# The value projections of the last four mLSTM heads as seven products of 2x2 blocks in seven PSUM banks

## The chip, the cores and the metric

One core of one Trainium2 chip runs the whole kernel. The metric is the device time of one execution in microseconds. Times of single instructions come from one profiled execution. PE is TensorE, DVE is VectorE, ACT is ScalarE; PSUM, the memory that TensorE writes, has eight banks of 128 x 512 float32.

## The reference, cut to what matters

The model is a two-layer trunk over 512 tokens of width 2048: an mLSTM layer, then a layer of band attention. The change lies in the mLSTM layer, whose input projection feeds eight heads.

```python
h = modulate(rmsnorm(x, g_pre[l]), shift, scale)          # (512, 2048)
proj = h @ w_in                                            # all columns of the layer
qk = silu(causal_conv(proj[..., :A_V0], conv_w, conv_b))   # queries and keys, 256 columns a head each
v = proj[..., A_V0:A_O0]                                   # values, 512 columns a head
o = proj[..., A_O0:A_Z0]
z = proj[..., A_Z0:A_G0]
ht = mlstm_chunkwise(heads(q), heads(k), heads(v), li, lf)  # scores, weights, weights @ values, per head
y = sigmoid(o) * rmsnorm(ht, g_head) * silu(z)
return y @ w_out
```

For one head the values are `h` (512 x 2048) times 512 columns of `w_in`. That product is what the change computes in another way.

## The kernel before, in words

**Numbers.** Everything is float32. A matmul operand is split into a high part (a cast to the rounded matmul type, made by ACT) and a low part (the rest, one subtraction on DVE); `split`, line 203, makes both. `mm3` makes one product of three matmuls: high x high, high x low, low x high. All matmuls are issued at line 272.

**Weights.** They lie in DRAM in the order in which the kernel uses them, which `stream()` writes out: a list of pieces of up to 128 x 1024. `raw_load` brings a piece into one of three raw buffers (`wr`, 512 KB, on the SP queue). `wpiece` (line 232 on) takes the next piece and makes `wh` and `wl` from it, three buffers each. If it is asked for sums, it first makes sums and differences of the piece's 2x2 blocks (`ws`, lines 242 to 244: one subtraction of 512, an addition and a subtraction of 256 columns in a piece of two pairs) and splits these too (`wsh`, `wsl`, 768 columns, two buffers each).

**Seven products.** The tiles of `proj_s` (a head's two query tiles, its two key tiles, each gate tile of o with that of z, keys of the attention layer) treat two k-tiles, two column tiles and two token halves as 2x2 blocks and form their product with seven block products in place of eight. Four banks D, C, A, B gather them. The block sums of the input `h1` (`h1s`, made by `three_sums`) exist from head 3 on; the sum for the first of a pair's tiles overwrites the second half of `h1` itself. At the end, lines 366 to 375 empty the banks: one copy on ACT from D, then four additions of 256 and one of 512 and one of 256 columns on DVE.

**A head from the fifth on (h > HALF, heads 4 to 7).** In this order on TensorE: a tile pair of queries (`ps_dzq`, `ps_czq`, `ps_azq`, `ps_bzq`), a pair of keys, the values, four tile pairs of the gates (`zo`), the normaliser (`ps_d`) and the weighted values (`ps_n`), whose matmuls mix with those of the next head. Queries and keys go through the convolution (`cv`, three DVE steps each, lines 656 to 661) and are split (`qk`).

**The values.** `proj_b` makes four banks of 128 tokens x 512 columns (`ps_v`): the token tile is stationary, 512 weight columns move. There are eight weight pieces, each of two k-tiles. Since `h1` holds a sum in its second token half, `wpiece` makes one difference of the two k-tiles' weights (`diff`, line 249, 512 columns) for these heads, and the second k-tile's products for the token blocks 2 and 3 use it. While the values run, four scores (`scores`, `ps_s`) are computed at given places (`at`), each in one bank of the second pool; DVE empties each at line 738 or 743. The values' banks are then split into `v` 0 to 2 (high by ACT, low by DVE, straight from PSUM) and copied to `v` 3.

**Banks.** Two pools share the eight banks: `newp` has five (psP), `newa` three (psA). A tile's name does not bind it to a bank; the recording layer gives it a bank that is free in its pool. `other` in `proj_s` says whether C, A and B come from `newa`.

**Order.** A scheduler puts the instructions of each engine in an order when the program is built; each engine then works through its own queue in that order and waits on semaphores. `tc.high_priority(AHEAD)` draws instructions forward: weight pieces and the emptying of banks have it, the convolutions of heads 4 to 7 have not.

Of the kernel before, what the change touches and what calls it, by code (L numbers as in the profile page):

```python
# [15 lines left out]
P = 128  # L16
D = 2048
# [27 lines left out]
RAMP = [4, 5, 6, 7]  # L45
HALF = 3
ATT_PAIRS = 8


def pair_pieces(f, merged=False):  # L50
# [22 lines left out]
def stream():  # L73

    out = []

    def add(mat, kts, cs):
        out.append((mat, [(k, c, n) for k in kts for c, n in cs]))

    def tile_a(mat, col, kts=KT):  # L80
        for k in range(0, kts, 8):
            add(mat, range(k, k + 8), [(col, P)])

    def tile_b(mat, col, kts=KT):
        for k in range(0, kts, 2):
            add(mat, [k, k + 1], [(col, 512)])

    def tile_s(mat, c1, c2, f, merged=False):
        for sk, nk in pair_pieces(f, merged):
            blocks = [(2 * k + i, c, P) for ks in sk for i, c in ((0, c1), (0, c2), (1, c2), (1, c1)) for k in ks]  # L90
            out.append((mat, blocks + [(2 * k + i, c, P) for k in nk for i in range(2) for c in (c1, c2)]))

    for step in first_steps():
        if len(step) == 1:
            add("a_w_in", step, [(c, P) for c in LEAD])
        else:
            k0, k1, i, g = step
            add("a_w_in", range(k0, k1), [(c, P) for c in LATER[i : i + g]])
    for h in range(NH):
        for c in (h * DK, V0 // 2 + h * DK):  # L100
            if 1 < h <= HALF:
                tile_a("a_w_in", c)
                tile_a("a_w_in", c + P)
            elif h > HALF:
                tile_s("a_w_in", c, c + P, HEAD_PAIRS, True)
        tile_b("a_w_in", V0 + h * DV)
        if h >= HALF:
            for i in range(4):
                tile_s("a_w_in", O0 + h * DV + i * P, Z0 + h * DV + i * P, HEAD_PAIRS if h > HALF else RAMP[i], True)
        elif h:  # L110
            for c0 in (O0, Z0):
                for i in range(4):
                    tile_a("a_w_in", c0 + h * DV + i * P)
    tile_b("a_w_out", 0, 32)
    for _ in PAIRS:
        for g in range(1, 4):
            tile_b("a_w_out", g * 512, 32)
    for _ in PAIRS:
        for g in range(2):
            tile_b("kv_w", D + g * 512)  # L120
    for i in range(KT // 2):
        tile_s("kv_w", 2 * i * P, (2 * i + 1) * P, KEY_PAIRS[i], True)
    for g in range(2, 4):
        tile_b("kv_w", D + g * 512)
    for h in range(BH):
        tile_s("b_w_in", h * P, D + h * P, ATT_PAIRS, True)
    for g in range(3):
        tile_b("b_w_out", g * 512)
    for _ in PAIRS:
        tile_b("b_w_out", 3 * 512)  # L130
    return out
# [15 lines left out]
def hybrid_trunk(ctx, tc, xT, xN, c, adaT, cols, wst, wg, ext, kc, out):  # L147
# [71 lines left out]
        keep(nc.sync.dma_start(raw, wst[at : at + P * n].rearrange("(p n) -> p n", p=P)))  # L219
        loads.append(raw)  # L220

    def wpiece(mat, groups=(), pl=None, bufs=(2, 2), diff=False, early=False):

        if stock and not early:
            return stock.pop(0)()
        i = wpos[0] - len(loads)
        m, blocks = order[i]
        assert m == mat  # L230
        n = sum(w for _, _, w in blocks)
        with tc.high_priority(ahead[0]):
            if not loads:
                raw_load()
            raw = loads.pop(0)
            ts = []
            c0 = 0
            for j, ns in enumerate(groups):
                w = ns * P
                r = raw[:, c0 : c0 + 4 * w]  # L240
                t = pl.tile([P, 3 * w], F32, tag="ws", name=f"ws{i}_{j}", bufs=bufs[0])
                nc.vector.tensor_tensor(t[:, : 2 * w], r[:, w : 3 * w], r[:, : 2 * w], op=ALU.subtract)  # L242
                nc.vector.tensor_tensor(r[:, w : 2 * w], t[:, w : 2 * w], r[:, :w], op=ALU.add)  # L243
                nc.vector.tensor_tensor(t[:, 2 * w :], r[:, 3 * w :], r[:, w : 2 * w], op=ALU.subtract)  # L244
                ts.append(t)
                c0 += 4 * w
            if diff:
                t = pl.tile([P, n // 2], F32, tag="ws", name=f"ws{i}", bufs=2)
                nc.vector.tensor_tensor(t, raw[:, n // 2 :], raw[:, : n // 2], op=ALU.subtract)
                ts.append(t)  # L250
            hi = wp.tile([P, 1024], F32R, tag="hi", name=f"wh{i}")[:, :n]
            lo = wp.tile([P, 1024], F32R, tag="lo", name=f"wl{i}")[:, :n]
            if i == 0:
                pin(nc.scalar.copy(hi, raw))

                def rest():
                    parted[0] = nc.vector.tensor_tensor(lo, raw, hi.bitcast(F32), op=ALU.subtract)
                    behind(parted[0], first[0])
                    return [(hi, lo)]

                return rest
            parted[:] = split(hi, lo, raw, *first[1:] if i < 3 else ())
            out = [(hi, lo)]
            for j, t in enumerate(ts):
                sh = pl.tile(list(t.shape), F32R, tag="wsh", name=f"wsh{i}_{j}", bufs=bufs[1])
                sl = pl.tile(list(t.shape), F32R, tag="wsl", name=f"wsl{i}_{j}", bufs=bufs[1])
                split(sh, sl, t)
                out.append((sh, sl))
        return out
# [20 lines left out]
    def proj_a(mat, xs, ps, t0=0, t1=S):  # L290
        proj(mat, xs, [ps], 8, 0, len(xs), len(xs) - 1, t0, t1)

    def proj_b(mat, xs, pss, ms=range(4), kts=KT, at={}, late=0, summed=0, pl=None):

# [1 line left out]
        for k0 in range(0, kts, 2):  # L298
            if k0 in at:
                at[k0]()  # L300
            held.append((k0, wpiece(mat, pl=pl, diff=k0 < 2 * summed)))
            if k0 >= kts - 2 * late and k0 < kts - 2:
                continue
            for group in [[pm] for pm in zip(pss, ms)] if k0 in (0, kts - 2) else [list(zip(pss, ms))]:
                for ka, parts in held:
                    for j in range(2):
                        k = ka + j
                        x = xs(k) if callable(xs) else xs[k]
                        for ps, m in group:
                            t = slice(m * P, (m + 1) * P)  # L310
                            other = j == 1 and m > 1 and len(parts) > 1
                            w = slice(0, 512) if other else slice(j * 512, (j + 1) * 512)
                            hi, lo = parts[other]
                            mm3(ps, x[:, 0, t], x[:, 1, t], hi[:, w], lo[:, w], k == 0, k == kts - 1)
            held.clear()

    def proj_s(mat, xs, ss, f, z1, z2, name, pl, bufs, at={}, merged=False, other=False):

        D, C, A, B = [(newa if other and n != "d" else newp)(f"ps_{n}{name}") for n in "dcab"]
        pieces = pair_pieces(f, merged)
        begun = set()
        h0, h1_ = slice(0, 256), slice(256, 512)
# [40 lines left out]
        with tc.high_priority(AHEAD):  # L365
# [7 lines left out]
                nc.vector.tensor_tensor(z2, z2, B.rearrange("p (a t) -> p a t", a=2), op=ALU.add)  # L373
            else:
                nc.vector.tensor_tensor(z2[:, 0, :], z2[:, 0, :], B[:, h0], op=ALU.add)

    def half_sums(raw, pl, tag, name, bufs, keep=lambda ins: ins):

# [334 lines left out]
            raw.append(r)  # L713
        h1s.append(three_sums(raw, hq, f"h1s{k}", HEAD_PAIRS, h1[2 * k][:, :, 256:]))

    def pair(c, name, other, f=HEAD_PAIRS, at={}):
        z1, z2 = (acp.tile([P, 2, 256], F32, tag="so", name=f"{name}_{i}", bufs=6) for i in range(2))
        proj_s("a_w_in", h1, h1s, f, z1, z2, name, hq, (2, 2), at, True, other)
        return [z.rearrange("p a t -> p (a t)") for z in (z1, z2)]

    def scores(h, j, qk, pr, nm, nmd, tot):
# [30 lines left out]
    for h in range(NH):  # L752
# [4 lines left out]
        for i in range(4):  # L757
            if h > HALF:
                if i % 2 == 0:
                    zs = pair((i // 2) * (V0 // 2) + h * DK, f"zq{h}_{i}", i > 0)  # L760
                ps = zs[i % 2]
            elif h < 2:
                ps = (lead, qk1)[h][i]
# [28 lines left out]
            add_at(at, {k: lambda: background(2) for k in ((4, 10) if h == 0 else (2, 6, 12))})  # L792
        if h == HALF:
            add_at(at, {k: head_sums for k in (2, 6, 10, 14)})
        pv = [newp(f"ps_v{h}_{m}") for m in range(4)]
        proj_b("a_w_in", h1, pv, at=at, summed=HEAD_PAIRS if h > HALF else 0, pl=hq if h > HALF else None)
        for i in (2 * h, 2 * h + 1):
            pin(nc.sync.dma_start(bsc[i], ext[i].partition_broadcast(P)))
        if h == 0:
# [4 lines left out]
        for m in range(4):  # L804
            with tc.high_priority(AHEAD):
                if m < 3:
                    t = hp.tile([P, 2, S], F32R, tag="qk", name=f"v{h}_{m}", bufs=4)
                    split(t[:, 0, :], t[:, 1, :], pv[m])
                else:
                    t = hp.tile([P, S], F32, tag="nm", name=f"v{h}_{m}")  # L810
                    nc.scalar.copy(t, pv[m])
# [5 lines left out]
        for i in range(4):  # L817
            if h >= HALF:
                f = HEAD_PAIRS if h > HALF else RAMP[i]
                o, sz = pair(O0 + h * DV + i * P, f"zo{h}_{i}", i % 2 == 0, f, {1: head_sums} if len(h1s) == f < HEAD_PAIRS else {})  # L820
                nc.scalar.activation(o, o, AF.Sigmoid)
                nc.scalar.activation(sz, sz, AF.Silu)
                nc.vector.tensor_tensor(o, o, sz, op=ALU.mult)
# [273 lines left out]
    for i in range(KT // 2):  # L1097
# [1 line left out]
        ready = len(hs)  # L1099
        at = {2: input_sums} if ready < KT // 2 else {}  # L1100
        assert ready == KEY_PAIRS[i]
        proj_s("kv_w", hkv, hs, ready, z[:, 0:2, :], z[:, 2:4, :], f"k{i}", zx, (2, 2), at, True, i % 2 == 1)
        nc.sync.dma_start(ksc[i].rearrange("p a t -> p (a t)"), z.rearrange("p a t -> p (a t)"))
    zxst.close()
    kst.close()
# [281 lines left out]
```

## Time and profile before

| | |
|---|---|
| median of 3 runs | 2770.73 us (2770.47 to 2773.43) |
| the profiled execution | 2771.84 us, of which the span of the trace is 2770.1 us |
| granted TensorE clock | 0.999 |
| one head's period, from the values of head 5 to those of head 6 | 1003.2 to 1180.0 us of the span, 176.8 us |
| matmuls in the span | 16402, with as many weight loads |

A row of the timeline begins with its start and its length in us, then engine, line, operation, output<-inputs, shapes; a bracket tells how long the engine had been idle before it and who ended that. A row of a chain has start, length, and the number of instructions that it stands for. A matmul's listed length is longer than the distance to the next one, since matmuls are pipelined; the spacing of starts tells what a product occupies.

### The profile page before, as it was taken

The numbers are of one execution on the slowest core, as the hardware profiler recorded it, in microseconds if no ns is written. First come the engines' busy times: TensorE is split into PE (matmuls) and PEld (weight loads), VectorE is DVE, ScalarE is ACT, GpSimd is POOL, SyncE is SP. The second block draws the span as 40 slices with busy tenths as digits, with TensorE's granted clock in tenths as the row PEclk, the third lists the DMA queues.
The fourth block names the chain that finished last, engine by engine and source line by source line (L and its number), as shares of the span: only waits on it lengthen the run. The fifth ranks groups of instructions, "written<-read, shape, count | busy, mean of one in ns | idle before, by whom it ended". The sixth has DMA issues, their size and how long they took to land.

```text
span 2770.1 us, 42407 instructions
## 1 busy us (share of the span) xinstructions
PE 2749.6 (99%) x16402; PEld 2451.6 (89%) x16402; DVE 2199.7 (79%) x3438; ACT 1399.4 (51%) x2000; POOL 0.2 (0%) x4
## 2 busy tenths in 40 slices
PE   8999999999999999999999999999999999999998
PEld 6887888888998999989999888887998899999877
DVE  8975978769997888978887677467976788899666
ACT  4243624234555555556555334468534466666523
POOL 0000000000000000000000000000000000000000
PEclk9999999999999999999999999999999999999999
DMA  9754687855233333333326699788535544444687
GB/s 368 292 204 131 249 301 259 312 202 204 101 114 107 99 124 100 115 103 105 124 94 221 223 297 310 237 273 279 176 129 189 169 129 129 126 123 126 211 311 243
DMA packets 167876, 527.08 MB, mean 190 GB/s; under 512 B 17989, under 2 KB 33893, under 8 KB 155001
## 3 DMA queue, kind: packets, MB, share of 16 engines
q1 hardware_dynamic: 167674, 524.38, 56.1%
q8 instruction: 128, 2.10, 0.3%
q14 instruction: 74, 0.61, 0.1%
HBM read 490.69 MB, written 38.85 MB: 191 GB/s over the span
## 4 chain that ended last, share of the span: by engine, by line
PE 93%; DVE 3%; DMA 2%; issue 1%; ACT 1%; SPq 0%; DVEq 0%; ACTq 0%
PE ps_y L272 18%; PE ps_v L272 12%; PE ps_kv L272 4%; PE ps_azo L272 4%; PE ps_o L272 4%; PE ps_czo L272 4%; PE ps_dzo L272 4%; PE ps_az L272 3%; PE ps_cz L272 3%; PE ps_dz L272 3%; PE ps_qk L272 3%; PE ps_z L272 3%; PE ps_l L272 3%; PE ps_bzo L272 2%; PE ps_s L272 2%; PE ps_n L272 2%
## 5 line engine op out<-in xcount | busy, mean ns | idle before, releaser
L203 DVE TENSOR_TENSOR wl<-wr,wh 128x1024 fp32r<-128x1024 f32 (+1 forms) x560 | 673.8, 1206 | 290.6 <-ACT wh L203 288.8
L203 ACT CAST wh<-wr 128x1024 fp32r<-128x1024 f32 (+1 forms) x560 | 579.8, 1037 | 625.5 <-PE ps_y L272 233.1
L272 PE MATMUL ps_y<-wh,y 128*128 128x512 f32 x1536 | 476.3, 390 | 0.0
L203 ACT CAST wsh<-ws 128x768 fp32r<-128x768 f32 (+2 forms) x240 | 189.1, 788 | 394.6 <-issue 170.3
L272 PEld LDWEIGHTS ps_y<-wh,y 128*128 128x128 f32 x1536 | 288.1, 188 | 59.3
L272 PE MATMUL ps_y<-wl,y 128*128 128x512 f32 x768 | 299.0, 389 | 0.0
L203 DVE TENSOR_TENSOR wsl<-ws,wsh 128x768 fp32r<-128x768 f32 (+2 forms) x240 | 215.3, 897 | 104.5 <-ACT wsh L203 102.5
L272 PE MATMUL ps_v<-wh,h 128*128 128x512 f32 x896 | 285.4, 390 | 0.0
L443 DVE CUSTOM_DVE_ANT_0 ada<-ada,scB,cl 128x2048 f32<-128x2048 f32 (+1 forms) x96 | 222.5, 2324 | 13.6 <-DMA ada<-in_adaT 13.6
L272 PEld LDWEIGHTS ps_v<-wh,h 128*128 128x128 f32 x896 | 168.2, 188 | 34.4
L272 PE MATMUL ps_v<-wl,h 128*128 128x512 f32 x448 | 174.7, 390 | 0.0
L272 PEld LDWEIGHTS ps_y<-wl,y 128*128 128x128 f32 x768 | 144.2, 188 | 29.8
L272 PE MATMUL ps_kv<-wh,hkv 128*128 128x512 f32 x512 | 159.4, 390 | 0.0
L242 DVE TENSOR_TENSOR ws<-wr 128x512 f32<-128x512 f32 (+1 forms) x208 | 138.9, 668 | 4.1 <-DMA wr<-in_wst 3.9
L272 PEld LDWEIGHTS ps_kv<-wh,hkv 128*128 128x128 f32 x512 | 96.1, 188 | 19.7
L272 PE MATMUL ps_kv<-wl,hkv 128*128 128x512 f32 x256 | 100.0, 390 | 1.4 <-DVE wl L203 1.4
L272 PEld LDWEIGHTS ps_v<-wl,h 128*128 128x128 f32 x448 | 84.2, 188 | 17.4 <-issue 0.9
L272 PE MATMUL ps_l<-h,wh 128*128 128x512 f32 x320 | 98.4, 390 | 0.0
L244 DVE TENSOR_TENSOR ws<-wr 128x256 f32<-128x256 f32 (+1 forms) x208 | 85.8, 413 | 3.4
L243 DVE TENSOR_TENSOR wr<-ws,wr 128x256 f32<-128x256 f32 (+1 forms) x208 | 85.4, 411 | 2.6
L272 PE MATMUL ps_qk<-h,wh 128*128 128x512 f32 x256 | 79.3, 390 | 0.0
L272 PE MATMUL ps_o<-h,wh 128*128 128x512 f32 x256 | 79.2, 389 | 0.0
(405 smaller groups left out, 6411.7 us busy)
## 6 DMA issues: line engine op xcount, KB each, us to landing
wr<-in_wst SPq DMA_DIRECT2D x530, 512.0 KB, 3.7
ada<-in_adaT SPq DMA_DIRECT2D x94, 1024.0 KB, 6.1
ada<-in_adaT SPq DMA_DIRECT2D x36, 512.0 KB, 6.3
adq<-in_adaT SPq DMA_DIRECT2D x64, 256.0 KB, 5.0
xt<-nsc SPq DMA_DIRECT2D x48, 256.0 KB, 4.3
wr<-in_wst SPq DMA_DIRECT2D x26, 384.0 KB, 3.3
yr<-ysc SPq DMA_DIRECT2D x28, 256.0 KB, 5.3
bsc<-in_ext SPq DMA_DIRECT2D x16, 320.0 KB, 6.1
```

The source lines that it names most:

```text
L203: ins = nc.scalar.copy(hi, src), nc.vector.tensor_tensor(lo, src, hi.bitcast(F32), op=ALU.subtract)
L242: nc.vector.tensor_tensor(t[:, : 2 * w], r[:, w : 3 * w], r[:, : 2 * w], op=ALU.subtract)
L243: nc.vector.tensor_tensor(r[:, w : 2 * w], t[:, w : 2 * w], r[:, :w], op=ALU.add)
L244: nc.vector.tensor_tensor(t[:, 2 * w :], r[:, 3 * w :], r[:, w : 2 * w], op=ALU.subtract)
L272: return nc.tensor.matmul(ps, a, b, start=start, stop=stop)
L443: pin(nc.vector.tensor_tensor_reduce(c, c, (sc or scB)[:, j * w : (j + 1) * w], 1.0, mod[:, i : i + 1] if j else col(CB + i), ALU.mult, AL ...
```

## The change: what it does

In heads 4 to 7 the values go through a new function, `proj_v`, in place of `proj_b`:

- the two k-tiles of a piece, the two halves of the 512 value columns and the two halves of the tokens are the 2x2 blocks; each block product is 128 tokens (stationary) by 256 columns (moving), with seven products in place of eight;
- 128 tokens of each half make one sub-block b; its banks are D, C, A, and both sub-blocks share a bank E, one half each: seven banks. Those of sub-block 0 and E come from `newp`, and so does C of sub-block 1; D and A of sub-block 1 come from `newa`, so that one bank is left for the four scores;
- the first two pieces and the last two are held: sub-block 0 takes both, then sub-block 1;
- `wpiece` makes the three block sums of a tile pair for each piece, and the difference of line 249 goes;
- the banks are emptied by additions into SBUF tiles, and `split` then reads these; `v` 3 is written directly;
- the score places move from k-tile 8, 10, 12, 14 to piece 4, 5, 6, 7, which is the same place in the stream;
- the four banks of a gate pair in these heads come from the pools as `OZ_BANKS` says.

```diff
+BANKS = ("pppp", "paaa")
+OZ_BANKS = ("pppa", "aapp", "paaa", "pppp")
...
+    def tile_v(mat, col):
+        for k in range(0, KT, 2):
+            c1, c2 = col, col + 256
+            out.append((mat, [(k + i, c, 256) for i, c in ((0, c1), (0, c2), (1, c2), (1, c1))]))
...
-        tile_b("a_w_in", V0 + h * DV)
+        if h > HALF:
+            tile_v("a_w_in", V0 + h * DV)
+        else:
+            tile_b("a_w_in", V0 + h * DV)
...
-            if diff:
-                t = pl.tile([P, n // 2], F32, tag="ws", name=f"ws{i}", bufs=2)
-                nc.vector.tensor_tensor(t, raw[:, n // 2 :], raw[:, : n // 2], op=ALU.subtract)
-                ts.append(t)
...
+    def proj_v(mat, xs, ss, zs, name, pl, bufs, at={}):
+        h0, h1_ = slice(0, 256), slice(256, 512)
+        E = newp(f"ps_e{name}")
+        banks = [[new(f"ps_{n}{name}_{b}") for n, new in zip("dca", news)] for b, news in enumerate(([newp] * 3, [newa, newp, newa]))]
+        begun = set()
+        n = KT // 2
+        held = []
+        def products(b, k, main, extra):
+            D, C, A = banks[b]
+            tok = slice(b * P, (b + 1) * P)
+            for ps, half, parts, blk, x in (
+                (D, 1, main, 1, ss[k][1]),
+                (D, 0, main, 0, xs[2 * k][:, :, h0]),
+                (C, 0, extra, 1, ss[k][2]),
+                (C, 1, extra, 0, ss[k][0]),
+                (A, 0, main, 3, xs[2 * k + 1][:, :, h0]),
+                (A, 1, main, 2, ss[k][3]),
+                (E, b, extra, 2, xs[2 * k + 1][:, :, h1_]),
+            ):
...
+                mm3(ps[:, h1_ if half else h0], x[:, 0, tok], x[:, 1, tok], parts[0][:, w], parts[1][:, w], start, bool(last))
+        def empty(b):
+            D, C, A = banks[b]
+            z0, z1 = zs(b)
+            f0, f1 = h0, h1_
+            with tc.high_priority(AHEAD):
+                nc.scalar.copy(z0[:, f0], D[:, h0])
+                nc.vector.tensor_tensor(z1[:, f1], z0[:, f0], D[:, h1_], op=ALU.add)
+                nc.vector.tensor_tensor(z1[:, f0], z1[:, f1], C[:, h0], op=ALU.add)
+                nc.vector.tensor_tensor(z0[:, f1], z1[:, f1], C[:, h1_], op=ALU.add)
+                nc.vector.tensor_tensor(z1[:, f1], z1[:, f0], C[:, h1_], op=ALU.add)
+                nc.vector.tensor_tensor(z0, z0, A, op=ALU.add)
+            return z0, z1
+        out = []
+        for k in range(n):
+            if k in at:
+                at[k]()
+            held.append((k, *wpiece(mat, [2], pl, bufs)))
+            if k in (0, n - 2):
+                continue
+            for b in range(2):
+                for piece in held:
+                    products(b, *piece)
+                if k == n - 1:
+                    out.append(empty(b))
+            held.clear()
+        for z, e in zip(out, (h0, h1_)):
+            with tc.high_priority(AHEAD):
+                nc.vector.tensor_tensor(z[1][:, h0], z[1][:, h0], E[:, e], op=ALU.add)
+        return [z[a] for a in range(2) for z in out]
...
+        if h > HALF:
+            def rows_of(b):
+                t = [acp.tile([P, S], F32, tag="so", name=f"zv{h}_{b}_{a}", bufs=6) for a in range(2 - b)]
+                return t + [hp.tile([P, S], F32, tag="nm", name=f"v{h}_3")] if b else t
+            pv = proj_v("a_w_in", h1, h1s, rows_of, f"v{h}", hq, (2, 2), {k // 2: f for k, f in at.items()})
+        else:
+            pv = [newp(f"ps_v{h}_{m}") for m in range(4)]
+            proj_b("a_w_in", h1, pv, at=at)
...
+                elif h > HALF:
+                    t = pv[m]
...
-                o, sz = pair(O0 + h * DV + i * P, f"zo{h}_{i}", i % 2 == 0, f, ...)
+                o, sz = pair(O0 + h * DV + i * P, f"zo{h}_{i}", OZ_BANKS[i] if h > HALF else BANKS[1 - i % 2], f, ...)
```

In the built program TensorE has 576 matmuls more (336 for 192 in each of four heads), DVE 112 instructions more (28 a head), and the order on every engine is the same as before outside the stretch from the values of head 4 to the first gate pairs of head 7. The tiles of the value stage are called `ps_dv`, `ps_cv`, `ps_av`, `ps_ev` and `zv`.

More of the change, by code (lines that the diff above doesn't have):

```diff
@@ L220, in raw_load, with wpiece @@
         loads.append(raw)
-    def wpiece(mat, groups=(), pl=None, bufs=(2, 2), diff=False, early=False):
+    def wpiece(mat, groups=(), pl=None, bufs=(2, 2), early=False):
         if stock and not early:
@@ L291, in proj_a, with proj_b @@
         proj(mat, xs, [ps], 8, 0, len(xs), len(xs) - 1, t0, t1)
-    def proj_b(mat, xs, pss, ms=range(4), kts=KT, at={}, late=0, summed=0, pl=None):
+    def proj_b(mat, xs, pss, ms=range(4), kts=KT, at={}, late=0):
         held = []
@@ L300, in proj_b @@
                 at[k0]()
-            held.append((k0, wpiece(mat, pl=pl, diff=k0 < 2 * summed)))
+            held.append((k0, wpiece(mat)))
             if k0 >= kts - 2 * late and k0 < kts - 2:
@@ L304, in proj_b @@
             for group in [[pm] for pm in zip(pss, ms)] if k0 in (0, kts - 2) else [list(zip(pss, ms))]:
-                for ka, parts in held:
+                for ka, [(hi, lo)] in held:
                     for j in range(2):
@@ L310, in proj_b, with proj_s @@
                             t = slice(m * P, (m + 1) * P)
-                            other = j == 1 and m > 1 and len(parts) > 1
-                            w = slice(0, 512) if other else slice(j * 512, (j + 1) * 512)
-                            hi, lo = parts[other]
+                            w = slice(j * 512, (j + 1) * 512)
                             mm3(ps, x[:, 0, t], x[:, 1, t], hi[:, w], lo[:, w], k == 0, k == kts - 1)
             held.clear()
-    def proj_s(mat, xs, ss, f, z1, z2, name, pl, bufs, at={}, merged=False, other=False):
-        D, C, A, B = [(newa if other and n != "d" else newp)(f"ps_{n}{name}") for n in "dcab"]
+    def proj_s(mat, xs, ss, f, z1, z2, name, pl, bufs, at={}, merged=False, banks="pppp"):
+        D, C, A, B = [(newa if b == "a" else newp)(f"ps_{n}{name}") for n, b in zip("dcab", banks)]
         pieces = pair_pieces(f, merged)
@@ L375, in proj_s @@
                 nc.vector.tensor_tensor(z2[:, 0, :], z2[:, 0, :], B[:, h0], op=ALU.add)
+    def proj_v(mat, xs, ss, zs, name, pl, bufs, at={}):
[17 more added lines that the diff above has]
+            ):
+                start = id(ps) not in begun
+                begun.add(id(ps))
+                w = slice(blk * 256, (blk + 1) * 256)
+                last = k == n - 1 and (b if ps is E else ps is not D and half or ps is D and not half)
+                mm3(ps[:, h1_ if half else h0], x[:, 0, tok], x[:, 1, tok], parts[0][:, w], parts[1][:, w], start, bool(last))
[28 more added lines that the diff above has]
+        return [z[a] for a in range(2) for z in out]
@@ L714, in head_sums, with pair @@
         h1s.append(three_sums(raw, hq, f"h1s{k}", HEAD_PAIRS, h1[2 * k][:, :, 256:]))
-    def pair(c, name, other, f=HEAD_PAIRS, at={}):
+    def pair(c, name, banks, f=HEAD_PAIRS, at={}):
         z1, z2 = (acp.tile([P, 2, 256], F32, tag="so", name=f"{name}_{i}", bufs=6) for i in range(2))
-        proj_s("a_w_in", h1, h1s, f, z1, z2, name, hq, (2, 2), at, True, other)
+        proj_s("a_w_in", h1, h1s, f, z1, z2, name, hq, (2, 2), at, True, banks)
         return [z.rearrange("p a t -> p (a t)") for z in (z1, z2)]
@@ L759, in hybrid_trunk @@
                 if i % 2 == 0:
-                    zs = pair((i // 2) * (V0 // 2) + h * DK, f"zq{h}_{i}", i > 0)
+                    zs = pair((i // 2) * (V0 // 2) + h * DK, f"zq{h}_{i}", BANKS[i // 2])
                 ps = zs[i % 2]
@@ L794, in hybrid_trunk @@
             add_at(at, {k: head_sums for k in (2, 6, 10, 14)})
-        pv = [newp(f"ps_v{h}_{m}") for m in range(4)]
-        proj_b("a_w_in", h1, pv, at=at, summed=HEAD_PAIRS if h > HALF else 0, pl=hq if h > HALF else None)
+        if h > HALF:
[6 more added lines that the diff above has]
+            proj_b("a_w_in", h1, pv, at=at)
         for i in (2 * h, 2 * h + 1):
@@ L819, in hybrid_trunk @@
                 f = HEAD_PAIRS if h > HALF else RAMP[i]
-                o, sz = pair(O0 + h * DV + i * P, f"zo{h}_{i}", i % 2 == 0, f, {1: head_sums} if len(h1s) == f < HEAD_PAIRS else {})
+                o, sz = pair(O0 + h * DV + i * P, f"zo{h}_{i}", OZ_BANKS[i] if h > HALF else BANKS[1 - i % 2], f, {1: head_sums} if len(h1s) == f < HEAD_PAIRS else {})
                 nc.scalar.activation(o, o, AF.Sigmoid)
@@ L1101, in hybrid_trunk @@
         assert ready == KEY_PAIRS[i]
-        proj_s("kv_w", hkv, hs, ready, z[:, 0:2, :], z[:, 2:4, :], f"k{i}", zx, (2, 2), at, True, i % 2 == 1)
+        proj_s("kv_w", hkv, hs, ready, z[:, 0:2, :], z[:, 2:4, :], f"k{i}", zx, (2, 2), at, True, BANKS[i % 2])
         nc.sync.dma_start(ksc[i].rearrange("p a t -> p (a t)"), z.rearrange("p a t -> p (a t)"))
```

## The prediction

> **What bounds the kernel now.** I read the page first, then the busy time by windows, then the chain of waits, then the timeline of VectorE at the place that changes.
>
> ```profile
> span 2770.1 us, 42407 instructions
> PE 2749.6 (99%) x16402; PEld 2451.6 (89%) x16402; DVE 2199.7 (79%) x3438; ACT 1399.4 (51%) x2000; POOL 0.2 (0%) x4
> ```
>
> TensorE is busy for 99% of the span. The change sits in heads 4 to 7, so the windows of one such head (head 5) count more than the mean: its queries and keys, its values, its gates, and one whole period from value stage to value stage.
>
> ```profile
> core 0: us, PE busy (x) PEld busy (x) DVE busy (x) ACT busy (x) POOL busy (x), PEclk, DMA share, GB/s
> 960.00:1003.20 43.20, 43.20 (x353) 42.85 (x353) 40.76 (x61) 23.04 (x31) 0.00 (x0) 1.00 0.34 112
> 1003.20:1051.00 47.80, 47.80 (x221) 39.98 (x220) 36.45 (x58) 28.55 (x41) 0.00 (x0) 1.00 0.36 113
> 1051.00:1132.00 81.00, 81.00 (x674) 80.87 (x673) 68.20 (x108) 42.52 (x51) 0.00 (x0) 1.00 0.32 105
> ...
> 1003.20:1180.00 176.80, 176.80 (x1274) 168.15 (x1273) 149.76 (x232) 98.85 (x127) 0.00 (x0) 1.00 0.34 109
> ```
>
> In each row PE is busy for the whole stretch at granted clock 1.00: a head takes 176.8 us because its matmuls do. Fewer columns shorten it at once, as long as nobody makes PE wait. Next is VectorE (DVE): 40.76 of 43.20 us with queries and keys, 36.45 of 47.80 with the values. ScalarE and DMA are far from full.
>
> **What the products save.** The chain of waits is here simply PE's queue, so its starts give the spacing of products.
>
> ```profile
> 365.66 43.53 PE ps_z L272 x192
> ...
> 1055.76 1.44 PE ps_dzo L272 x12
> ...
> 1060.80 1.44 PE ps_dzo L272 x12
> ```
>
> 192 products of 512 columns take 43.53 us, 226.7 ns each. Between the two ps_dzo rows lies one weight piece of a gate tile pair: 42 products of 256 columns (seven products of three matmuls, two pairs) in 5.04 us, 120 ns each. A value projection is now 16 k-tiles x 4 token blocks x 3 = 192 wide products, 43.53 us. It becomes 8 pairs x 2 token sub-blocks x 7 x 3 = 336 narrow ones, 40.32 us. Saved: 3.21 us a head, 12.8 us over four heads. The new products have the gates' shape (128x128 stationary, 256 moving, one weight load each); that tokens are now stationary and weights moving shows no price in the rows, so I take 120 ns.
>
> From those two spacings, 256 columns cost 106.7 ns and the instruction 13.3 ns more. The Trainium skill, "TensorE: Matmul & The Clock Gate", section "Wait — 56ns, not 53.3ns?", puts that fixed cost at about 2.5 ns. By it, as an estimate, a value stage would fall from 41.4 to 36.7 us and the saving would be 18.9 us. The trace disagrees with 13.3 ns, and I keep the trace.
>
> **What VectorE gets.** Here are its starts around the beginning of head 5's value products, whose first one PE starts at 1003.07.
>
> ```profile
> 1003.07 0.40 PE L272 MATMUL ps_v<-wh,h 128*128 128x512 f32 x1
> ```
>
> ```profile
> 994.87 1.22 DVE L203 TENSOR_TENSOR wl<-wr,wh 128x1024 fp32r<-128x1024 f32 x1
> 996.01 0.95 DVE L203 TENSOR_TENSOR wsl<-ws,wsh 128x768 fp32r<-128x768 f32 x1
> 996.87 0.74 DVE L658 SCALAR_TENSOR_TENSOR cv<-zq,cl,cv 128x509 f32<-128x509 f32 x1
> 997.54 0.68 DVE L249 TENSOR_TENSOR ws<-wr 128x512 f32<-128x512 f32 x1
> 998.14 0.68 DVE L203 TENSOR_TENSOR wsl<-ws,wsh 128x512 fp32r<-128x512 f32 x1
> 998.74 0.74 DVE L658 SCALAR_TENSOR_TENSOR cv<-zq,cl,cv 128x511 f32<-128x511 f32 x1
> ...
> 1001.30 0.41 DVE L368 TENSOR_TENSOR zq<-zq,ps_czq 128x256 f32<-128x256 f32 x1
> 1001.64 0.41 DVE L369 TENSOR_TENSOR zq<-zq,ps_czq 128x256 f32<-128x256 f32 x1
> 1001.97 1.22 DVE L203 TENSOR_TENSOR wl<-wr,wh 128x1024 fp32r<-128x1024 f32 x1
> 1003.10 0.41 DVE L370 TENSOR_TENSOR zq<-zq,ps_czq 128x256 f32<-128x256 f32 x1
> 1003.43 0.41 DVE L375 TENSOR_TENSOR zq<-zq,ps_bzq 128x256 f32<-128x256 f32 x1
> 1003.76 0.68 DVE L371 TENSOR_TENSOR zq<-zq,ps_azq 128x512 f32<-128x512 f32 x1
> 1004.36 0.68 DVE L203 TENSOR_TENSOR wsl<-ws,wsh 128x512 fp32r<-128x512 f32 x1
> ```
>
> With a full queue the next one starts about 0.08 us before the last has ended. What an operation occupies is therefore the distance of starts: 1.13 us for 1024 columns, 0.86 for 768, 0.60 for 512, 0.34 for 256, 0.67 for a step of the convolution.
>
> Each of eight value pieces loses one subtraction of 512 (0.60) and gets the three of a tile pair (0.60 + 0.34 + 0.34); its split of the sums grows from 512 to 768 columns (0.60 to 0.86). That is 0.94 us a piece, 7.5 us a head. Emptying the seven banks adds ten operations of 256 and two of 512, 4.6 us; the three splits that make hi and lo of the values stay. So DVE gets 12.1 us more: some 162 of 173.6 us, 93%. On average it fits, so the cost lies where the work bunches.
>
> **Where it bunches.** The scheduled order of the changed program is the same in all four heads but for bank numbers. I count from V, the first value product. On DVE, behind the emptying of the keys (its last starts at 1003.76, the next operation at 1004.36, V + 1.29), stand until the last key split is done: five splits of 1024 (5.65 us), five of 768 (4.30), five subtractions of 512 (3.00), nine operations of 256 (3.06), ten convolution steps (6.70) and four query and key splits (2.40). Sum 25.1 us, so V + 26.4; up to the third of the four splits V + 25.2. Some 0.7 us of waiting for ScalarE's casts comes on top (the second query split and the next weight split stand just behind their casts): V + 25.9 and V + 27.1.
>
> PE's order puts the first score behind 199 narrow products (23.9 us). Its third matmul, the first to need the third split, stands at V + 25.4, its sixth, which needs the fourth, at V + 26.7. PE waits about 0.6 us at the third, hand-over included; the sixth then just fits. Before, this place had room:
>
> ```profile
> 1017.81 1.29 DVE L203 TENSOR_TENSOR qk<-cv,qk 128x512 fp32r<-128x512 f32 x2 [0.39 <-ACT qk L203]
> 1019.34 1.23 DVE L203 TENSOR_TENSOR wl<-wr,wh 128x1024 fp32r<-128x1024 f32 x1 [0.24 <-ACT wh L203]
> ```
>
> ```profile
> 1024.86 1.53 PE L272 MATMUL ps_s<-qk,qk 128*128 128x512 f32 x6
> ```
>
> The last key split ended at 1019.1, the score began at 1024.86: 5.8 us of slack, and the new order uses up all of it.
>
> The second place is the score bank. Seven value banks leave one for four scores, where before they went through three; each score must wait until DVE has taken the one ahead. A hand-over by itself is short:
>
> ```profile
> 1026.53 0.68 DVE L738 SCALAR_TENSOR_TENSOR e<-ps_s,e 128x512 f32<-128x512 f32 x1
> ```
>
> ```profile
> 1027.30 0.62 ACT L203 CAST p<-e 128x512 fp32r<-128x512 f32 x1 [1.62 <-DVE e L738]
> 1030.52 1.06 ACT L203 CAST wh<-wr 128x1024 fp32r<-128x1024 f32 x1 [2.59 <-PE ps_v L272]
> ```
>
> The score ended at 1026.39, DVE took it at 1026.53, ScalarE followed 0.09 us behind DVE. So a score's bank is free 0.9 us after its end if DVE is free. The order leaves 1.2 us of other products between scores one and two, 3.5 between two and three, 1.8 between three and four. The fourth is the tight one: its predecessor's emptying stands on DVE behind the 1024 split of the next gate piece, which waits for ScalarE's cast (1.06 us), which waits for a buffer that PE frees at V + 32.3. That gives 32.3 + 0.1 + 1.06 + 0.1 + 1.13 + 0.34 + 0.1 = V + 35.1, and PE wants the bank at V + 35.15. I allow 0.2 us. A further 0.1 goes to the third value piece's sums: the count of DVE's operations reaches their split at V + 10.0, which with 0.86 and a hand-over makes V + 11.0, and PE wants it at V + 11.2. Together 0.9 us a head.
>
> **What costs nothing, and what hides it.** The first two and the last two pieces are held together, so the second is wanted 2.5 us behind the first instead of 5; its split is 1.2 us ahead by the same count. The first token sub-block's banks are emptied while PE runs the second (5.04 us) and 4.6 us of emptying is spread over that and the first gate piece; the gate's first banks come from the first sub-block, its last one from the scores, and its second tile pair, 20 us on, takes the rest. The later gate pairs find banks that stood idle for a tile. If that cover goes, the price is the emptying of one sub-block, about 2.3 us a head. ScalarE gets 0.21 us for each of eight wider casts, and two copies of 256 for one of 512: 2 us beside 28.55 of 47.80. Bytes, loads and their count stay; the position-bias copies move by some places in the load queue, with DMA at 0.36. Each raw tile is now changed in place before its cast, but three raw buffers and a 512 KB load per 5 us leave that slack. Everything outside heads 4 to 7 keeps its order.
>
> **Sum.** 12.8 saved, 4 x 0.9 = 3.6 given back: 9.2 us. The profiled execution took 2771.84 us (span 2770.1), so its like would take 2762.6; the median of the runs, 2770.73, goes to 2761.5. Bounds of the waits: nothing (2757.9), and, if DVE overlapped nothing and each operation cost its whole row, 38 operations x 0.08 = 3.0 us more in the bunch and about 1 us from the stretch before it, 4.9 us a head (2777.5). A gain beyond 12.8 is excluded, since PE has no idle time in a head that could go. I take 0.9, near the lower end, since the spacing of full-queue rows is what the same operations show at this very place.
>
> **Rivals.**
>
> *DVE pays whole durations.* The row speaks against it: 0.68 us operations start 0.60 us apart. The Trainium skill, "VectorE: DVE Perf Modes", section "The DRAIN you can't avoid", says the next operation does not start until the pipe is empty. As a mechanism here: lateness 0.9 + 3.0 to 0.9 + 4.0 us a head, 2773.5 to 2777.5. Chance 0.03.
>
> *DVE's bunch is partly worse than counted.* Casts and splits alternate between ScalarE and DVE, and each crossing can leave DVE idle for some tenths (0.24 and 0.39 in the rows above). With 1.8 to 4.6 us a head the gain is eaten: 2765.2 to 2776. For it: no slack is left in 26 us. Against: 0.7 us of such waits are in the sum, and PE's own wait gives DVE time. Chance 0.12.
>
> *The single score bank stalls PE (slower).* If DVE is behind, a score's emptying stands behind a 1024 and a 768 split, 2.0 us, and PE behind the next score. Three hand-overs make 6 us a head: 4 x (6 - 3.2) = 11 us, about 2782. It decides from 4.6 us a head on. Against: other products are placed between the scores. Chance 0.10.
>
> *The narrow products cost more than 120 ns with the tokens stationary*, or the change is not what it says. At 135 ns the stage takes 45.4 us: 4 x 1.8 + 3.6 = 11 us slower, about 2782. The matching shapes speak against it. Chance 0.03.
>
> *The products cost less*, by the fixed cost of a few nanoseconds: four value stages would lose up to 18.9 us, 2755.4 with my waits. The 13.3 ns contradict it. Chance 0.02.
>
> **How the numbers follow.** The forecast, waits below 1.8 us a head, gets the rest, 0.70, and the time 2761.5. 0.2% is 5.5 us, about what a measurement of this kernel can tell from no change. Faster than 2765.2: 0.70 + 0.02 = 0.72. Same: 0.12 and most of 0.03, 0.14. Slower: 0.14. The range runs from 2757.5 (no waits) to 2774, which takes in most of the second rival and leaves out the score bank, dearer products, whole durations and the cheaper products, 0.18 in all. The forecast's own range is 2757.9 to 2765.
>
> **What would show it.** Right: a head's period near 174.5 us; 336 products of 256 columns 120 ns apart; PE idle of under 2 us a head, nearly all of it ahead of ps_s, released by DVE's qk; DVE without a gap for about 26 us from the start of the value products. Wrong: PE waiting for wl or wsl of a value piece, for e at each score, or at the first gate pair for a bank; a spacing other than 120 ns; changes outside heads 4 to 7.

## The result, and the profile after

The changed kernel takes 2759.61 us (median of five runs, 2758.69 to 2761.86), the kernel before 2770.73 us: 11.1 us less, a ratio of 0.996 with a 95% interval of 0.9945 to 0.9974. The forecast was 2761.5 us. The profiled execution took 2759.61 us, 12.2 us less than the profiled one before.

The page of the changed kernel, and its windows for head 5 in the order of those before (queries and keys, values, gates, a whole period):

```profile
span 2757.8 us, 43681 instructions
PE 2737.7 (99%) x16978; PEld 2470.2 (90%) x16978; DVE 2239.4 (81%) x3550; ACT 1402.6 (51%) x2002; POOL 0.2 (0%) x4
```

```profile
core 0: us, PE busy (x) PEld busy (x) DVE busy (x) ACT busy (x) POOL busy (x), PEclk, DMA share, GB/s
957.30:1000.50 43.20, 43.20 (x354) 42.86 (x353) 40.93 (x63) 21.06 (x28) 0.00 (x0) 1.00 0.36 118
1000.50:1045.00 44.50, 44.50 (x361) 43.96 (x361) 42.06 (x72) 30.30 (x43) 0.00 (x0) 1.00 0.29 103
1045.00:1126.00 81.00, 81.00 (x676) 80.96 (x675) 72.27 (x119) 42.71 (x52) 0.00 (x0) 1.00 0.32 111
1000.50:1174.40 173.90, 173.90 (x1418) 172.54 (x1418) 160.05 (x260) 99.23 (x127) 0.00 (x0) 1.00 0.32 111
```

The period of a head fell from 176.8 to 173.9 us and PE stayed at the top of every row. DVE went from 36.45 of 47.80 us to 42.06 of 44.50 us in the value stage, and from 149.76 to 160.05 us in a period. Four heads by 2.95 us, the difference of head 5's value stages below, make 11.8 of the 12.2 us.

The chain of waits of the changed kernel is PE's queue, as before; start, length, count. The ps_n rows are the weighted values, once in each head:

```profile
956.50 3.62 PE ps_n L278 x22
...
1000.62 0.72 PE ps_dv L278 x6
...
1015.74 0.72 PE ps_dv L278 x6
...
1018.26 0.72 PE ps_dv L278 x6
...
1044.81 0.36 PE ps_ev L278 x3
1045.17 1.44 PE ps_dzo L278 x12
...
1130.37 3.62 PE ps_n L278 x22
```

From the ps_dv row at 1015.74 to the one at 1018.26, 21 products of 256 columns, it is 2.52 us: 120 ns each, with the tokens stationary too. No gap stands in front of the first gate pair (the ps_dzo row). The same stage in the chain before, from its first value product to its first gate product:

```profile
1003.23 21.80 PE ps_v L272 x96
...
1050.73 1.43 PE ps_dzo L272 x12
```

The gaps are where the scores are. PE's timeline of the same execution (start, length; the first row is the first value product):

```profile
1000.45 0.28 PE L278 MATMUL ps_dv<-wh,h1s 128*128 128x256 f32 x1
...
1025.75 0.28 PE L278 MATMUL ps_ev<-wsh,h 128*128 128x256 f32 x1
1026.03 0.97 PE L278 MATMUL ps_s<-qk,qk 128*128 128x512 f32 x3
1026.84 0.28 PE L278 MATMUL ps_ev<-wsl,h 128*128 128x256 f32 x1
...
1035.77 0.28 PE L278 MATMUL ps_av<-wh,h 128*128 128x256 f32 x1
1035.91 0.98 PE L278 MATMUL ps_s<-qk,qk 128*128 128x256 f32 x6
1036.73 0.28 PE L278 MATMUL ps_av<-wh,h1s 128*128 128x256 f32 x1
```

The product at 1025.75 occupies 0.12 us, and the third score matmul starts 0.28 us behind it: 0.16 us of waiting. The three score matmuls should occupy 0.68 us and take 0.81: another 0.13. A third gap lies in the fourth score (1035.91), whose six matmuls of 256 columns should occupy 0.72 us and take 0.82: 0.10. That is 0.39 us in this head, and 0.38 to 0.43 in the other three. The second gap lies behind the wait and not in front of it; the trace does not say why. DVE at the same places:

```profile
1001.59 0.95 DVE L213 TENSOR_TENSOR wsl<-ws,wsh 128x768 fp32r<-128x768 f32 x1
...
1011.42 0.69 DVE L213 TENSOR_TENSOR qk<-cv,qk 128x512 fp32r<-128x512 f32 x1 [0.22 <-ACT qk L213]
...
1025.29 0.68 DVE L213 TENSOR_TENSOR qk<-cv,qk 128x512 fp32r<-128x512 f32 x1
1025.90 0.68 DVE L252 TENSOR_TENSOR ws<-wr 128x512 f32<-128x512 f32 x1
1026.50 0.68 DVE L213 TENSOR_TENSOR qk<-cv,qk 128x512 fp32r<-128x512 f32 x1
1027.10 0.41 DVE L253 TENSOR_TENSOR wr<-ws,wr 128x256 f32<-128x256 f32 x1
...
1035.44 0.42 DVE L802 SCALAR_TENSOR_TENSOR e<-ps_s,e 128x256 f32<-128x256 f32 x1
```

From 1001.59 to 1027.10, 25.5 us, the only idle time for which the trace names a cause (the bracket) is 0.22 us. The last row empties the bank of the third score; it ends at 1035.86, 0.05 us before the fourth score starts in the one bank left for scores. Counted from the first value product, the third query and key split, a key's, makes way for the next operation at V + 25.5 and the fourth at V + 26.7, where the prediction had V + 25.9 and V + 27.1.

### The profile page after: what moved, and what is told of

It is laid out like the page before. It is cut to its first block, busy times and chain, and to the rows that moved or that the text cites. A ratio compares the mean times of both kernels' runs of the same rounds, so it can differ in the third digit from the quotient of the medians.

```text
span 2757.8 us, 43681 instructions
## 1 busy us (share of the span) xinstructions
PE 2737.7 (99%) x16978; PEld 2470.2 (90%) x16978; DVE 2239.4 (81%) x3550; ACT 1402.6 (51%) x2002; POOL 0.2 (0%) x4
## 4 chain that ended last, share of the span: by engine, by line
PE 91%; DVE 4%; DMA 3%; issue 1%; ACT 1%; SPq 0%; DVEq 0%; ACTq 0%
PE ps_y L278 16%; PE ps_v L278 6%; PE ps_azo L278 4%; PE ps_o L278 4%; PE ps_kv L278 4%; PE ps_czo L278 4%; PE ps_dzo L278 4%; PE ps_az L278 3%; PE ps_cz L278 3%; PE ps_dz L278 3%; PE ps_qk L278 3%; PE ps_z L278 3%; PE ps_l L278 3%; PE ps_bzo L278 2%; PE ps_s L278 2%; PE ps_n L278 2%
## 5 line engine op out<-in xcount | busy, mean ns | idle before, releaser
L213 ACT CAST wsh<-ws 128x768 fp32r<-128x768 f32 (+1 forms) x240 | 195.8, 816 | 374.8 <-issue 135.3
L213 DVE TENSOR_TENSOR wsl<-ws,wsh 128x768 fp32r<-128x768 f32 (+1 forms) x240 | 223.6, 932 | 93.2 <-ACT wsh L213 90.9
L252 DVE TENSOR_TENSOR ws<-wr 128x512 f32<-128x512 f32 (+1 forms) x240 | 159.7, 670 | 3.5 <-DMA wr<-in_wst 3.3
L278 PE MATMUL ps_v<-wh,h 128*128 128x512 f32 x512 | 160.6, 390 | 0.0
L278 PEld LDWEIGHTS ps_v<-wh,h 128*128 128x128 f32 x512 | 96.1, 188 | 19.7
L254 DVE TENSOR_TENSOR ws<-wr 128x256 f32<-128x256 f32 (+1 forms) x240 | 98.1, 413 | 2.8
L278 PE MATMUL ps_v<-wl,h 128*128 128x512 f32 x256 | 100.0, 391 | 0.0
L253 DVE TENSOR_TENSOR wr<-ws,wr 128x256 f32<-128x256 f32 (+1 forms) x240 | 97.7, 411 | 2.1
L278 PE MATMUL ps_z<-h,wh 128*128 128x512 f32 x256 | 78.8, 389 | 0.0
```

What stands on the lines that cost most here:

```text
L213: ins = nc.scalar.copy(hi, src), nc.vector.tensor_tensor(lo, src, hi.bitcast(F32), op=ALU.subtract)
L278: return nc.tensor.matmul(ps, a, b, start=start, stop=stop)
```

## The experiments

Theory: the time falls by the columns that PE no longer streams, less a short wait at the first score, which comes from a VectorE queue without slack up to that point. Rivals: the gain, or the waits, come from the dealing of banks or the order around it; VectorE sets the pace by now; VectorE has slack, and the waits are a matter of order alone.

**Two heads instead of four** (heads 4 and 5 keep `proj_b`, its difference and the old gate banks):

```diff
-        if h > HALF:   # tile_v, proj_v, v 3, OZ_BANKS
+        if h > 5:
```

> The new value stage in heads 6 and 7 alone; heads 4 and 5 keep the 192 wide products and the old gate banks. Theory (the time falls by the columns that TensorE no longer streams, less a wait of about 0.4 us a head at the first score): half the gain, 5.5 to 6 us, so 2765 us; heads 4 and 5 keep a period of 176.8 us, head 6 shows 173.9. Rival (the gain comes from the changed order around the heads, not from the products): no proportion, all of it or none.

It took 2765.77 us, a ratio of 0.998 (0.9971 to 0.9989): half of the gain. The chain's rows for the weighted values stand once in each head:

```profile
955.11 3.62 PE ps_n L282 x22
...
1131.91 3.62 PE ps_n L282 x22
...
1305.75 3.62 PE ps_n L282 x22
```

176.80 us with wide products in head 5, 173.84 us with narrow ones in head 6. The gain is made per head, as the sum has it.

**The gate banks of before:**

```diff
-OZ_BANKS[i] if h > HALF else BANKS[1 - i % 2]
+BANKS[1 - i % 2]
```

> The changed kernel with the gate pairs' banks dealt as before (first pair: D from the five, C, A and B from the three). Theory: the first pair's A then waits for the bank of the second sub-block's D and its B for that sub-block's A, which DVE has emptied about 2 and 0.8 us before PE wants them: at most 0.3 us a head, 2759.5 to 2761. Rival (the new dealing is needed to keep the gain): about 3 us a head, the emptying of a sub-block, so 2771.

2760.07 us, ratio 0.9961 (0.9949 to 0.9974): the same as the changed kernel. Its trace has no gap in front of the first gate pair of a head either. The value banks are emptied in time for this dealing as well, as the theory had it; the new dealing is no part of the gain.

**An eighth product** (C's first product added twice, 48 matmuls more a head):

```diff
                 (C, 0, extra, 1, ss[k][2]),
+                (C, 0, extra, 1, ss[k][2]),
```

> The changed kernel with an eighth narrow product a piece and sub-block (the first of C's is added twice, so the values are not the reference's): 48 matmuls more a head. Theory (TensorE's columns set the time): 48 x 0.120 = 5.8 us a head, less the wait of 0.4 us at the first score, which the slower value stage covers: 21 to 23 us, 2781 us, about 10 us above the kernel before. Rival (VectorE sets the value stage's time by now): the added products lie beside its work, under 12 us, 2771 at most.

2781.64 us, ratio 1.0039 (1.0026 to 1.0051), within the theory's numbers. The chain's rows in the same places:

```profile
961.77 3.62 PE ps_n L278 x22
...
1141.18 3.62 PE ps_n L278 x22
```

A period is 179.41 us, 5.54 more than 173.87 in the changed kernel; 48 x 0.120 is 5.76, and the gaps at the scores fall from 0.39 to 0.20 us a head. So every added column was paid for and PE still sets the pace, with DVE at 92% of a period in the changed kernel.

**More VectorE work:**

```diff
                 nc.vector.tensor_tensor(t[:, : 2 * w], r[:, w : 3 * w], r[:, : 2 * w], op=ALU.subtract)
+                if twice:   # value pieces of heads 4 to 7
+                    nc.vector.tensor_tensor(t[:, : 2 * w], r[:, w : 3 * w], r[:, : 2 * w], op=ALU.subtract)
```

> The changed kernel, in which each value piece of heads 4 to 7 makes its subtraction of 512 columns twice (8 x 0.60 = 4.8 us more VectorE work a head, the result the same). Theory (VectorE has no slack in the 26 us before the first score): five of the doubled operations lie in that bunch and three just before it, so the key splits come 3 to 4.4 us later and PE waits that much longer at the first score: 12 to 17 us, 2771 to 2777. Rival (VectorE has slack, the waits of 0.4 us come from something else): under 2 us, 2761.

2762.27 us, ratio 0.9967 (0.9955 to 0.9979), 2.7 us above the changed kernel: the theory's 12 to 17 us did not come, and the rival's bound of 2 us was nearer. But the order had moved. With the added work the scheduler put the scores elsewhere; PE's timeline of this run has the first score in two parts:

```profile
1028.08 0.66 PE L280 MATMUL ps_s<-qk,qk 128*128 128x512 f32 x2
```

Only two of its matmuls stand there, the other four run between 1029.9 and 1037.1 in this run's chain, spread over value products. So the run does not tell whether there was slack before the old place. Two more runs fix the place.

**Fixed places, and fixed places with more VectorE work.** An order on PE's queue alone, with no wait:

```diff
+            due = score_end[0] if k - 1 in at else None
...
+                if due is not None:
+                    behind(a, due)      # each product of this piece stands behind that score
```

> The changed kernel, in which the products of a value piece are ordered behind the score asked for one piece before, on TensorE's queue alone (no wait is added). In the built order the four scores stand where they stood, the second 0.6 us earlier. It is the other side of the next run. Both theories: as the changed kernel, 2759.5 to 2762.

> The doubled subtraction of each value piece (4.8 us more VectorE work a head) together with the fixed places of the scores, so that the order cannot move the scores behind the work, as it did where the subtraction was doubled alone. Theory (VectorE has no slack up to the first score, and only the place of the scores hid the added work there): the first score keeps its place 25.2 us into the value products, the key splits come 3 to 4.4 us later, and PE waits that much in front of it: 12 to 17 us above the run with fixed places, 2771 to 2777. Rival (VectorE has slack before the score too): under 2 us, 2763 at most.

The first took 2762.78 us, ratio 0.9973 (0.9964 to 0.9982), a little above the range expected: the second score, 0.6 us nearer to the first, waits a little for the bank, and heads 5 to 7 have 0.8 us of gaps each, which makes some 1.1 of the 3.2 us above the changed kernel; the rest is not explained. The second took 2809.86 us, ratio 1.0141 (1.0127 to 1.0155): 47 us more than with fixed places alone, from the same added work that cost 2.7 us when the scores could move. Its waits of PE in the four heads, and a period from its chain:

```profile
PE ps_s L281 <- ACT qk L213: 31.4, 8, 6.2
PE ps_s L281 <- DVE qk L213: 3.1, 4, 0.9
```

```profile
962.05 3.62 PE ps_n L281 x22
...
1149.39 3.62 PE ps_n L281 x22
```

PE waits for the parts of the keys (`qk`, the high parts from ACT and the low ones from DVE) and for nothing else of weight: there was no slack before the score. The size was off, 11.8 us a head in place of 3 to 4.4. The timelines of DVE and ACT in head 5 (value products begin at 1010.09) tell two parts:

```profile
1039.11 0.69 DVE L213 TENSOR_TENSOR qk<-cv,qk 128x512 fp32r<-128x512 f32 x1
1039.71 0.69 DVE L255 TENSOR_TENSOR ws<-wr 128x512 f32<-128x512 f32 x1
...
1046.77 0.69 DVE L213 TENSOR_TENSOR qk<-cv,qk 128x512 fp32r<-128x512 f32 x1 [1.85 <-ACT qk L213]
```

```profile
1041.42 1.04 ACT L213 CAST wh<-wr 128x1024 fp32r<-128x1024 f32 x1 [1.19 <-DVE wr L256]
1042.49 1.28 ACT L731 ACT_TABLE_LOAD   x1
1043.78 0.63 ACT L731 ACTIVATE cv<-cv 128x512 f32<-128x512 f32 x1
1044.43 1.28 ACT L806 ACT_TABLE_LOAD   x1
1045.72 0.51 ACT L806 ACTIVATE e<-nm,aT 128x256 f32<-128x256 f32 x1
1046.14 0.60 ACT L213 CAST qk<-cv 128x512 fp32r<-128x512 f32 x1
```

The third split makes way at V + 29.6 (1039.71), 4.2 us later than in the changed kernel, and PE waits 2.4 and 0.9 us up to that point: this part is as expected. The fourth does not start 1.2 us behind the third but 7.7, since its cast stands on ScalarE behind a weight cast and two table loads of 1.28 us around one activation; PE waits 6.1 us for it. The order on both engines changed with the load, so how much of those six and a half us the added work alone would have cost stays open. The third part is a slower PE behind the wait, shown in the last section.

**Scores one piece later:**

```diff
-{k // 2: f for k, f in at.items()}
+{5: at[8], 6: at[10], 7: lambda: (at[12](), at[14]())}
```

> The changed kernel with the four scores asked for one piece later (at pieces 5, 6, 7 and 7 in place of 4 to 7). In the built order the first score moves by 1.3 us, and the gaps between its followers become 3.9, 1.6 and 1.1 us where they were 0.6 to 1.2, 3.5 and 1.8. Theory: the wait of 0.3 us at the first score goes, and the last two scores wait for their one bank, 0.5 to 1 us a head: 2760 to 2763, the wait showing at the third and fourth ps_s. Rival (the scores are not where PE loses time): no change in either place.

2761.39 us, ratio 0.9965 (0.9952 to 0.9977). Of the gaps at the first score 0.11 to 0.16 us is left, and 0.17 us stands at a later one, less than the 0.5 to 1 expected:

```profile
951.96 3.62 PE ps_n L278 x22
...
1125.78 3.62 PE ps_n L278 x22
```

173.82 us a period, no difference from 173.87 that could be told. In either place the waits at the scores cost about 0.4 us a head at most.

**Convolutions drawn forward:**

```diff
-conv(ps, chs[i], f"{h}_{i}", 1 < h <= HALF)
+conv(ps, chs[i], f"{h}_{i}", 1 < h)
```

> The changed kernel with the convolutions of heads 4 to 7 drawn forward like the weight pieces, so that the query and key splits come ahead of weight splits on VectorE. Theory (VectorE's bunch is full, an order can only move the wait): the wait leaves the first score and turns up at the sums of the first value pieces, several us a head: 2763 to 2775. Rival (the 0.4 us a head are a matter of order alone): they go, 2758.

2766.22 us, ratio 0.9981 (0.9972 to 0.9991), inside the theory's numbers. But the wait did not go to the sums of the value pieces, as I had written; PE's timeline has most of it still at the first score, which the new order starts some 6 us into the value products:

```profile
1007.79 0.73 PE L278 MATMUL ps_s<-qk,qk 128*128 128x512 f32 x2 [1.15 <-ACT qk L213]
```

1.3 us there and 0.3 at a value product's low part. Of the orders tried, none beats the changed kernel's.

## Why the prediction was right

- *The columns.* 336 products at 120 ns came as written, and PE is still the bound (the eighth product). The value stage, from the first value product to the first gate product in the chain, took 47.50 us before (1003.23 to 1050.73) and 44.55 after (1000.62 to 1045.17), 2.95 us less; with 0.39 of waits that is 3.34 gross, where 3.21 was reckoned. The wide value products were a little dearer, 227.1 ns each in the row at 1003.23, than the gate products from which I took 226.7.
- *The fixed cost.* 256 columns cost 120 ns, so the 13.3 ns an instruction hold for the new products too. The estimate of 18.9 us from the 2.5 ns in the Trainium skill, "TensorE: Matmul & The Clock Gate", section "Wait — 56ns, not 53.3ns?", is not what the runs show.
- *The wait at the first score.* Right in place and cause; 0.29 us a head in place of 0.6. The term that was too large is the idle time of DVE between ScalarE's casts: 0.7 us reckoned, 0.22 us shown. The 25.1 us of work took 25.5 with all idle time in it, and began at V + 1.14, 0.15 earlier than counted.
- *The work of DVE.* 12.1 us a head more was reckoned; its busy time rose by 10.3. The share of a period, 93% reckoned and 92% shown, hardly differs.
- *The score bank.* 0.10 us a head in place of 0.2, at the score that was named. Later and closer scores still found their bank within 0.3 us.
- *The third value piece.* No gap; 0.1 was allowed.
- *What costs nothing.* The first gate pair waited for nothing, with either dealing of banks. Outside heads 4 to 7 the two profiled executions differ by 0.4 us in all: the value products of head 4 start 0.3 us later, and what follows the values of head 7 is 0.7 us shorter.
- *The rivals.* Whole durations of DVE: the rows at 1025.29, 1025.90 and 1026.50 are 0.60 apart for operations of 0.68, and with whole durations the splits would have been 3 us late. A partly worse bunch: not in the changed kernel, though the run with fixed places and more work shows how near it is. The single bank: not at 2 us a hand-over. Dearer products: not so, and cheaper ones neither, at 120 ns.

In all 0.9 us a head was allowed for waits and 0.39 came, and gross 0.13 more was saved: 0.64 us a head, 2.6 us in all, by which the forecast was too slow on the profiled executions (9.2 us for 11.8). That the median came within 1.9 us of the forecast is in part luck: the medians differ by 1.1 us less than the profiled executions do.

## What to carry to other kernels

Where PE has no idle time in a stage, price the columns from the spacing of starts, then write down what the next engine must have finished by when: one ledger, starts for costs, in the built order, told that 12 us of added VectorE work a head would cost under 1 us of waiting. Slack that a scheduler can find is not the slack of a fixed order: the same added work cost 2.7 us when the scores could move and 47 us when they could not, some 11 of them by a slower clock (next section). An experiment that adds work to a scheduled kernel has to hold the order, or it tests the scheduler.

## What the runs showed of the hardware

After its long wait in the run with fixed places and more work, PE did not go on at 120 ns. Its timeline:

```profile
1046.79 1.65 PE L281 MATMUL ps_s<-qk,qk 128*128 128x512 f32 x3 [6.14 <-ACT qk L213]
1048.24 0.41 PE L281 MATMUL ps_dv<-wh,h1s 128*128 128x256 f32 x1
1048.45 0.41 PE L281 MATMUL ps_dv<-wl,h1s 128*128 128x256 f32 x1
...
1053.05 0.28 PE L281 MATMUL ps_av<-wl,h 128*128 128x256 f32 x1
1053.16 0.28 PE L281 MATMUL ps_av<-wh,h 128*128 128x256 f32 x1
```

For some 6 us the products of 256 columns stand 0.21 us apart, then 0.12 again. The windows of that stretch give the granted clock, the third figure from the end:

```profile
1036.00:1038.90 2.90, 0.64 (x2) 0.30 (x2) 2.90 (x4) 2.87 (x5) 0.00 (x0) 1.00 0.78 239
1039.10:1046.70 7.60, 0.80 (x1) 0.29 (x1) 5.79 (x11) 6.02 (x8) 0.00 (x0) 0.50 0.28 105
1046.80:1052.60 5.80, 5.80 (x20) 5.24 (x21) 3.06 (x5) 1.77 (x4) 0.00 (x0) 0.50 0.00 1
```

The clock was already 0.50 when the wait of 6.14 us began. It fell at about 1039.1, behind a wait of 2.40 us that ended at 1038.26 and at the start of one of 0.86 us, and was 1.00 again from about 1052.8, 6.0 us after PE had gone on. The other three heads show the same, with 3.2 to 6.4 us at half clock behind the longest wait. Half of these 21 us in the four heads, some 11 of the 47 us, is an estimate of what that cost.

The Trainium skill, "TensorE: Matmul & The Clock Gate", section "What's actually happening", has a clock gate that falls to half rate after an idle window of about 3.4 us and opens again after one of sustained work. The trace agrees with the half rate, 0.50. But no wait before the fall was longer than 2.40 us in this head, or 2.74 us in head 4, and PE had worked for some 0.7 us between the two; and from PE's next matmul to the full clock it took 3.2 to 6.4 us. The single wait of 1.15 us in the run with the convolutions drawn forward left the clock at 0.999 in the mean.

So in this run a long wait of PE, 3 to 6 us, cost its length and 1.6 to 3.2 us behind it, by the same estimate. The waits of 0.2 us in the changed kernel cost theirs and 0.1 us behind them, with the clock at 1.00 through its value stage.
